# A batched matrix product with x loaded one group ahead, wide stores, and a group's two halves multiplied in two phases

## The chip, the cores and the metric

One core of a Trainium2 chip. The metric is the device time of one execution in microseconds. Kernels are compared with the kernel before on the same chip in the same rounds.

## The reference

```python
batch, dim_i, dim_j, dim_k = 32, 256, 512, 384
x = randn(batch, dim_i, dim_j)      # float32
y = randn(batch, dim_j, dim_k)      # float32
out = np.einsum('bij,bjk->bik', x, y)
```

41.9 MB are read and 12.6 MB written.

## The kernel before

The batch is cut into N = 8 groups of Q = 4 matrices (numbered 0 to 7). Each matrix occupies 32 partitions, so that each partition's data are one long run in HBM: 16 KB of x, 24 KB of y, and for the result 6 KB. Per group:

- VectorE casts x to fp16 and transposes it in 32x32 blocks (pairs of fp16 as one 32-bit word); it casts y in four pieces.
- TensorE multiplies on four row tiles of 32 partitions, one per matrix g. The 256 rows of each result are two halves e (even and odd rows). A group thus has 2 x 4 results of 128x384 fp32, each in one bank of PSUM, the memory that the matmuls write: eight banks, all there are.
- ScalarE copies the banks to SBUF, the memory that the stores read, where the rows get their place for the store. For the last group, VectorE takes half of the copies.

```python
x_pool, y_pool, xt_pool, yr_pool: bufs=2;  xr_pool: bufs=1;  o_pool: bufs=5
psum_pool = tile_pool(name="psum", bufs=2 * Q, space=PSUM)          # 8 banks

def multiply(n):                                                    # ... cut
    for a in range(0, T, 4):                      # four pieces of y, T = 16
        nc.vector.tensor_copy(y_r[:, a:a+4], y_sb[:, a:a+4])
        for e in range(NE):                       # both halves, piece by piece
            for t in range(a, a + 4):
                for g in range(Q):
                    matmul(ps_of[n][e][g], xt[s, e, t // 2, :, t % 2], y_r[s, t],
                           start=(t == 0), stop=(t == T - 1))

def collect(n):                                   # w = 64: 16 copies of 64x384
    for u in range(2):
        for e in range(NE):
            for v in range(2):
                for h in range(2):
                    copy(o[v*w:(v+1)*w, u, h*NE + e], ps_of[n][e][2*u + v][h*w:(h+1)*w])

for n in range(2): load(n)                        # x_n, then y_n
for n in range(N):
    transpose_x(n); multiply(n); collect(n)
    if n + 2 < N: load(n + 2)
    if 0 <= n - 1 and n + 2 < N: store(n - 1)     # two stores of 768 KB
for n in range(N - 3, N): store(n)
```

Every engine runs its instructions in the order of the program, and all transfers go through one queue in that order.

## Time and profile before

| kernel before | |
|---|---|
| time, median of 6 runs | 137.06 us (136.16 to 138.03) |
| profiled span | 135.5 us |
| DMA, VectorE, TensorE, ScalarE busy | 96%, 62%, 47%, 43% |
| data moved | 54.7 MB at 404 GB/s, 54.5 of them through the one queue |

(The prediction had the first three of these runs, median 136.62.) Two of the page's groups; the columns are busy time and the mean of one in ns, then the engine's idle time before it and what ended most of that.

```profile
L113 PE MATMUL o_ps<-y_r,xt_sb 32*128 32x384 f16 x1024 | 64.2, 415 | 62.9 <-DVE y_r L107 61.0
L139 ACT COPY o_sb<-o_ps 64x384 f32<-64x384 f32 x120 | 56.7, 473 | 71.6 <-PE o_ps L113 45.5
```

ScalarE spends 0.47 us on a copy and is idle for more than half of the span. TensorE waits for casts, and for ScalarE hardly at all: 1.8 us in the list of waits.

### The profile page before, as it was taken

How to read it: one execution, taken by the hardware profiler on the slowest of the kernel's cores; microseconds unless marked ns; L12 is line 12 of the kernel's file. 1: busy time of each engine (PE TensorE's matmuls, PEld its weight loads, DVE VectorE, ACT ScalarE, POOL GpSimd, SP SyncE). 2: the span in 40 equal slices, each digit the busy share in tenths (PEclk: the TensorE clock that was granted, in tenths of full speed). 3: DMA queues.
4: the chain of work that ended last, by engine and by line, in shares of the span. 5: the costliest groups of instructions: out<-in, count | busy, mean ns of one | idle time of the engine just before them, and what ended most of it. 6: DMA issues, size and time to landing. Idle time of an engine off the chain costs nothing.

```text
span 135.5 us, 2381 instructions
## 1 busy us (share of the span) xinstructions
PE 64.2 (47%) x1024; PEld 33.7 (25%) x1024; DVE 83.6 (62%) x80; ACT 58.0 (43%) x121; POOL 0.2 (0%) x4
## 2 busy tenths in 40 slices
PE   0000099309934793579408940099302970089500
PEld 0000056104612361136104520045101540045200
DVE  0049777947897596822979059670796509990660
ACT  3000000894089408940794079500795039800640
POOL 0000000000000000000000000000000000000000
PEclk9999999975797579757975698556985698556985
DMA  4999999999999998999999999999999999999765
GB/s 111 426 431 457 414 445 450 389 428 474 392 435 421 435 399 339 442 441 450 398 399 453 423 457 385 415 431 457 418 385 417 441 409 419 415 421 426 302 279 210
DMA packets 5050, 54.68 MB, mean 404 GB/s; under 512 B 560, under 2 KB 560, under 8 KB 3120
## 3 DMA queue, kind: packets, MB, share of 16 engines
q1 hardware_dynamic: 5040, 54.53, 96.2%
q8 instruction: 8, 0.13, 0.4%
q14 instruction: 2, 0.02, 0.0%
HBM read 41.94 MB, written 12.58 MB: 402 GB/s over the span
## 4 chain that ended last, share of the span: by engine, by line
DMA 76%; DVE 13%; PE 5%; SPq 1%; issue 1%; DVEq 1%
DMA x_sb<-in_x_dram 76%; DVE x_r L83 7%; PE o_ps L113 5%; DVE xt_sb L96 3%; DVE o_sb L137 3%; DVE y_r L107 1%; DVEq L192 0%; SPq L77 0%; SPq L67 0%; DVEq L83 0%; DVEq L137 0%; DVEq L96 0%
## 5 line engine op out<-in xcount | busy, mean ns | idle before, releaser
L113 PE MATMUL o_ps<-y_r,xt_sb 32*128 32x384 f16 x1024 | 64.2, 415 | 62.9 <-DVE y_r L107 61.0
L139 ACT COPY o_sb<-o_ps 64x384 f32<-64x384 f32 x120 | 56.7, 473 | 71.6 <-PE o_ps L113 45.5
L113 PEld LDWEIGHTS <-xt_sb 32*128 32x128 f16 x1024 | 33.7, 116 | 93.0 <-DVE y_r L107 46.6
L83 DVE CAST x_r<-x_sb 128x4096 f16<-128x4096 f32 x8 | 18.4, 2294 | 33.3 <-DMA x_sb<-in_x_dram 33.3
L107 DVE CAST y_r<-y_sb 128x1536 f16<-128x1536 f32 x32 | 28.5, 953 | 8.6 <-DMA y_sb<-in_y_dram 8.6
L96 DVE STREAM_TRANSPOSE xt_sb<-x_r 128x512 f32<-128x512 f32 x32 | 32.4, 1072 | 0.7
L137 DVE COPY o_sb<-o_ps 64x384 f32<-64x384 f32 x8 | 4.4, 556 | 5.0 <-PE o_ps L113 4.8
L139 ACT ACT_TABLE_LOAD x1 | 1.3, 1283 | 0.7 <-PEq L181 0.7
L181 POOL MEMSET const-bfloat16-1.0<- 128x1 bf16 x1 | 0.1, 101 | 0.0
L181 POOL MEMSET const-uint8-127<- 128x1 uint8 x1 | 0.1, 101 | 0.0
L181 POOL MEMSET const-float32-0.0<- 128x1 f32 x1 | 0.1, 99 | 0.2 <-issue 0.2
L181 POOL MEMSET const-float32-1.0<- 128x1 f32 x1 | 0.1, 98 | 0.0
## 6 DMA issues: line engine op xcount, KB each, us to landing
y_sb<-in_y_dram SPq DMA_DIRECT2D x7, 3072.0 KB, 25.5
x_sb<-in_x_dram SPq DMA_DIRECT2D x8, 2048.0 KB, 24.9
out_dram<-o_sb SPq DMA_DIRECT2D x16, 768.0 KB, 20.6
y_sb<-in_y_dram SPq DMA_DIRECT2D x4, 768.0 KB, 24.1
```

What stands on the lines that cost most here:

```text
L83: keep(nc.vector.tensor_copy(x_r, x_of.pop(n)))
L96: keep(nc.vector.transpose(dst[:, b, e], src[:, b, e]))
L107: keep(nc.vector.tensor_copy(y_r[:, a : a + step], y_sb[:, a : a + step]))
L113: nc.tensor.matmul(ps_of[n][e][g], xt[s, e, t // 2, :, t % 2], y_r[s, t], start=(t == 0), stop=(t == T - 1),)
L137: keep(nc.vector.tensor_copy(dst, src))
L139: keep(nc.scalar.copy(dst, src))
L181: nc = _bacc.Bacc("TRN2", target_bir_lowering=False, num_devices=1)
```

## The change

Its intent: get the transposes of x off the end of the kernel, and halve the number of packets of the stores. Three things change.

1. *x one group ahead.* The queue gets x of group n+3 before y of group n+2, and VectorE transposes group n+1 before it casts y of group n.
2. *12 KB stores for groups 0 to 5 ("wide").* All eight rows of a partition lie together; for that the copies are 32x384, 32 of them per group: 28 on ScalarE, the 4 of the last bank on VectorE.
3. *Two phases for the wide groups.* Half e=0 is multiplied over the whole of y, then e=1, and each half's four banks are copied when it is done. Groups 6 and 7 stay narrow and mixed, as before.

```diff
     def width(n):
-        return NARROW
+        return WIDE if n < N - 2 else NARROW
@@ the main loop (cut: load, multiply and collect are only split into parts)
-    for n in range(2):
-        load(n)
+    load_x(0); load_x(1); load_y(0); transpose_x(0); load_x(2); load_y(1)
     for n in range(N):
-        transpose_x(n)
-        multiply(n)
-        collect(n)
-        if n + 2 < N:
-            load(n + 2)
+        if n + 1 < N:
+            transpose_x(n + 1)
+        if n > 0 and width(n - 1) == WIDE:
+            collect(nc.vector.tensor_copy, n - 1, NE - 1, Q - 1)
+        round_y(n)
+        if width(n) == WIDE:
+            for e in range(NE):
+                multiply(n, e, 0, T)
+                for g in range(Q):
+                    if (e, g) != (NE - 1, Q - 1):
+                        collect(nc.scalar.copy, n, e, g)
+        else:
+            for a in range(0, T, STEP):
+                for e in range(NE):
+                    multiply(n, e, a, a + STEP)
+            ... # the copies of before, on VectorE for v == 1 of the last group
+        if n + 3 < N:
+            load_x(n + 3)
+        if n + 2 < N:
+            load_y(n + 2)
             ... # store(n - 1) as before
```

More of the change, by code (lines that the diff above doesn't have):

```diff
@@ L5 @@
 from concourse import bass_utils, mybir
-from concourse.masks import make_identity
 from concourse._compat import with_exitstack
@@ L19 @@
 DEFER = 3
+STEP = 4
 @with_exitstack
@@ L58, in width, with load_x @@
     def width(n):
-        return NARROW
-    def pieces(n):
-        return 4
-    def load(n):
+        return WIDE if n < N - 2 else NARROW
+    def load_x(n):
         x_of[n] = x_pool.tile([P, R, J], F32, name="x_sb")
@@ L71, in load, with load_y @@
         )
+    def load_y(n):
         y_of[n] = y_pool.tile([P, T, K], F32, name="y_sb")
@@ L96, in transpose_x, with round_y @@
                     keep(nc.vector.transpose(dst[:, b, e], src[:, b, e]))
-    def multiply(n):
-        xt = xt_of.pop(n).bitcast(MM_DT).rearrange("p e t (m c) -> p e t m c", c=2)
+    def round_y(n):
         y_sb = y_of.pop(n)
-        y_r = yr_pool.tile([P, T, K], MM_DT, name="y_r")
-        ps_of[n] = [
-            [psum_pool.tile([P, K], F32, name="o_ps") for _ in range(Q)] for _ in range(NE)
-        ]
-        step = T // pieces(n)
-        for a in range(0, T, step):
-            keep(nc.vector.tensor_copy(y_r[:, a : a + step], y_sb[:, a : a + step]))
-            for e in range(NE):
-                for t in range(a, a + step):
-                    for g in range(Q):
-                        s = slice(g * PQ, (g + 1) * PQ)
-                        keep(
-                            nc.tensor.matmul(
-                                ps_of[n][e][g],
-                                xt[s, e, t // 2, :, t % 2],
-                                y_r[s, t],
-                                start=(t == 0),
-                                stop=(t == T - 1),
-                            )
-                        )
@@ L122, in collect, with multiply @@
-    def collect(n):
+        yr_of[n] = yr_pool.tile([P, T, K], MM_DT, name="y_r")
+        for a in range(0, T, STEP):
+            keep(nc.vector.tensor_copy(yr_of[n][:, a : a + STEP], y_sb[:, a : a + STEP]))
+    def multiply(n, e, first, last):
+        xt = xt_of[n].bitcast(MM_DT).rearrange("p e t (m c) -> p e t m c", c=2)
+        if first == 0:
+            for g in range(Q):
+                ps_of[n, e, g] = psum_pool.tile([P, K], F32, name="o_ps")
+        for t in range(first, last):
+            for g in range(Q):
+                s = slice(g * PQ, (g + 1) * PQ)
+                keep(
+                    nc.tensor.matmul(
+                        ps_of[n, e, g],
+                        xt[s, e, t // 2, :, t % 2],
+                        yr_of[n][s, t],
+                        start=(t == 0),
+                        stop=(t == T - 1),
+                    )
+                )
@@ L123, in collect @@
+    def collect(copy, n, e, g):
         w = width(n)
         per = P // w
-        o_of[n] = o_pool.tile([P, R, K], F32, name="o_sb")
+        ps = ps_of.pop((n, e, g))
         o = o_of[n].rearrange("p (u f) k -> p u f k", u=Q // per)
-        for u in range(Q // per):
-            for e in range(NE):
-                for v in range(per):
-                    g = u * per + v
-                    ps = ps_of[n][e][g]
-                    on_vector = n == N - 1 and g % 2 == 1
-                    for h in range(per):
-                        src = ps[h * w : (h + 1) * w]
-                        dst = o[v * w : (v + 1) * w, u, h * NE + e]
-                        if on_vector:
-                            keep(nc.vector.tensor_copy(dst, src))
-                        else:
-                            keep(nc.scalar.copy(dst, src))
@@ L140, in collect @@
-        del ps_of[n]
+        for h in range(per):
+            keep(copy(o[g % per * w : (g % per + 1) * w, g // per, h * NE + e], ps[h * w : (h + 1) * w]))
     def store(n):
@@ L153, in store @@
             )
-    for n in range(2):
-        load(n)
-    for n in range(N):
-        transpose_x(n)
-        multiply(n)
-        collect(n)
+    load_x(0)
+    load_x(1)
+    load_y(0)
+    transpose_x(0)
+    load_x(2)
+    load_y(1)
+    for n in range(N):
+        if n + 1 < N:
+            transpose_x(n + 1)
+        if n > 0 and width(n - 1) == WIDE:
+            collect(nc.vector.tensor_copy, n - 1, NE - 1, Q - 1)
+        o_of[n] = o_pool.tile([P, R, K], F32, name="o_sb")
+        round_y(n)
+        if width(n) == WIDE:
+            for e in range(NE):
+                multiply(n, e, 0, T)
+                for g in range(Q):
+                    if (e, g) != (NE - 1, Q - 1):
+                        collect(nc.scalar.copy, n, e, g)
+        else:
+            for a in range(0, T, STEP):
+                for e in range(NE):
+                    multiply(n, e, a, a + STEP)
+            for u in range(2):
+                for e in range(NE):
+                    for v in range(2):
+                        on_vector = n == N - 1 and v == 1
+                        collect(nc.vector.tensor_copy if on_vector else nc.scalar.copy, n, e, 2 * u + v)
+        if n + 3 < N:
+            load_x(n + 3)
         if n + 2 < N:
-            load(n + 2)
-        if n + 2 - DEFER >= 0 and n + 2 < N:
-            store(n + 2 - DEFER)
+            load_y(n + 2)
+            if n + 2 - DEFER >= 0:
+                store(n + 2 - DEFER)
     for n in range(N - DEFER, N):
```

## The prediction

> **What bounds the kernel now.** I read the page first: the slices (part 2), the queues (part 3) and the chain of waits (part 4); then the timeline of the last 35 us.
>
> ```profile
> DMA  4999999999999998999999999999999999999765
> q1 hardware_dynamic: 5040, 54.53, 96.2%
> DMA 76%; DVE 13%; PE 5%; SPq 1%; issue 1%; DVEq 1%
> ```
>
> The reader is to see that the 16 DMA engines are busy from the second slice to the 37th, that the one queue fills 96.2% of their span, and that the chain is three quarters transfers. Only the head (2 us) and the last three slices (3.4 us each; 0.3 + 0.4 + 0.5 of one missing, some 4 us) hold idle DMA. So what can be won is small: the tail, and cheaper packets. What can be lost is larger: anything that makes compute follow the last loads later.
>
> ```profile
> 102.90 0.47 ACT L139 COPY o_sb<-o_ps 64x384 f32<-64x384 f32 x1
> 103.17 3.57 DVE L107 CAST y_r<-y_sb 128x1536 f16<-128x1536 f32 x4 [1.10 <-DMA y_sb<-in_y_dram]
> ...
> 104.19 6.87 PE L113 MATMUL o_ps<-y_r,xt_sb 32*128 32x384 f16 x128 [8.06 <-DVE y_r L107]
> 110.48 7.83 ACT L139 COPY o_sb<-o_ps 64x384 f32<-64x384 f32 x16 [7.11 <-issue]
> 111.82 2.29 DVE L83 CAST x_r<-x_sb 128x4096 f16<-128x4096 f32 x1 [5.09 <-DMA x_sb<-in_x_dram]
> 114.22 4.03 DVE L96 STREAM_TRANSPOSE xt_sb<-x_r 128x512 f32<-128x512 f32 x4
> 118.18 3.52 DVE L107 CAST y_r<-y_sb 128x1536 f16<-128x1536 f32 x4
> 119.15 7.91 PE L113 MATMUL o_ps<-y_r,xt_sb 32*128 32x384 f16 x128 [8.09 <-DVE y_r L107]
> 126.48 3.88 ACT L139 COPY o_sb<-o_ps 64x384 f32<-64x384 f32 x8 [8.18 <-issue]
> 126.54 4.56 DVE L137 COPY o_sb<-o_ps 64x384 f32<-64x384 f32 x8 [4.84 <-PE o_ps L113]
> ```
>
> This is the tail: groups 6 and 7 (counted from 0). ScalarE empties group 6 from 110.48 to 118.31; group 7's matmuls start at 119.15, held by VectorE (cast x, transpose, cast y), and only 0.8 us after the banks are free. From ScalarE's first copy of group 7 (126.48) to the end of the span (135.5) it is 9.0 us: copies to 131.1, the last store issued at 131.16, landed at 134.42, 1.06 us to finish.
>
> ```profile
> 44.64 0.47 PE L113 MATMUL o_ps<-y_r,xt_sb 32*128 32x384 f16 x1 [0.33 <-ACT o_sb L139]
> ...
> 45.62 6.48 PE L113 MATMUL o_ps<-y_r,xt_sb 32*128 32x384 f16 x109 [0.51 <-ACT o_sb L139]
> ...
> 51.33 7.83 ACT L139 COPY o_sb<-o_ps 64x384 f32<-64x384 f32 x16 [5.76 <-PE o_ps L113]
> ```
>
> Here, in an early group, the other regime shows itself: TensorE waits bank by bank for ScalarE, the last 109 matmuls start when the last of eight banks is copied (45.57), and ScalarE's next group begins 5.76 us after that. I use this number below.
>
> **What the Trainium skill says.** "DMA: Bandwidth & Descriptors", section "Why small descriptors are slow (HBM only)": each packet carries a fixed overhead. The trace's packet records agree: medians of 234 ns at 6,144 B, 611 at 16,384 and 912 at 24,576 fit 0.0368 ns per byte plus 8 ns. "PSUM — Partial Sum Buffer", section "Terms": one matmul output fits at most one of eight banks. Here each of a group's eight outputs takes one, so a group that mixes its halves fills all of PSUM; the waits at 44.64 and 45.62 agree. "ScalarE: Activation LUTs", section "What ACT_TABLE_LOAD costs": 186 ns + 0.833 N for an instruction with immediates, back-to-back ones overlapping by some 93 ns, with no term for partitions. For N = 384 that is 506, or 413 apart; the trace has 473, and 7.83/16 = 489 apart, which I use. So a 32-partition copy should cost what a 64-partition one does. "TensorE: Matmul & The Clock Gate", Part 1: an idle window brings the clock to half. The windows of the trace agree: 16 to 20 matmuls per us at granted clock 0.50, 32 at 1.00.
>
> **The change part by part.**
>
> 12 KB stores, groups 0 to 5. Removed: 6 x 256 = 1,536 packets of 6 KB; added: 768 of 12 KB. Saved: 768 x 8 ns / 16 engines = 0.4 us of DMA time, 0.06 per group. In a full queue this counts, but little.
>
> Copies. A wide group needs 8 outputs x 4 blocks = 32 copies of 32x384 where it had 16 of 64x384. VectorE takes 4 (2.25 us at 556 ns and a gap), ScalarE 28: 28 x 0.489 = 13.7 us, up from 7.83. VectorE per group: 2.3 cast + 4.05 transposes (two of twice the length, taken as the same) + 2.25 + 3.57 = 12.2 us, up from 9.9. DMA per group with stores is 7.5 (y) + 4.9 (x) + 3.7 (store) = 16.1 us, so both fit. The serial chain per group, first y cast 0.97 + matmuls 7.2 + transposes into the xt buffer just freed 4.05 + VectorE's copies 2.25 = 14.5, also fits. About 15 us of transfers remain queued in the worst early group (3), so the DMA stays full. Middle: nothing on the path.
>
> Two phases. They let the 28 copies run under the second half's matmuls, but group 6 is narrow: it mixes halves and uses all eight banks at once.
>
> x one group ahead. It moves x7's cast and transposes (6.3 us) out of the end. But x7 now passes the queue before y6: the transfers from x7 on are x7, y6, store 3, y7, store 4. Working back from y7, which landed at 119.26 (119.0 with the saving): minus 7.5 and 3.7, y6 lands at 107.8 (it was 103.14); minus 7.5, x7 at 100.3.
>
> The tail then goes: VectorE 100.3 + 2.3 + 4.05 + 2.25 (group 5's copies) = 108.9, later than y6's landing. First y6 cast 0.97: group 6's matmuls start at 109.9, against 104.19. ScalarE's copies of it begin some 7.2 later (6.3 to 7.5 in the profile), at 117.1. Group 5's 28 copies may hold them further: y5 cast from about 93 to 94, first half done 4.4 later, 13.7 of copies, done at 111 to 112; plus 5.76 gives 116.9 to 117.9. So 117.1 to 117.9. Group 7 needs all eight banks, and the last is free 7.83 later, at 124.9 to 125.7; +5.76 for matmuls to ScalarE's first copy, 130.7 to 131.5; +9.0 as before: span 139.7 to 140.5. The y7 casts, done by 120, no longer matter. The unprofiled median lies 1.1 above the profiled span (136.62 against 135.5); so 140.8 to 141.6. I predict 141.1 us, 3.3% more.
>
> In one sum: group 6's start +5.7, ScalarE's start on it +6.6 to +7.4, the gap from its last copy to group 7's first (8.17 before: 118.31 to 126.48) -2.4, hence +4.2 to +5.0 us.
>
> **The rivals.**
> A. The DMA stays the bound to the end. Stores 4, 5, 6, 7 would follow y7 without a hole: the slowest engine had landed group 6's at 130.37; plus 2 x 1.85 minus 0.4 gives 133.7, plus 1.06: span 134.7, time 135.8, 0.6% faster. For it: the x chain does leave the end. Against it: it needs group 7's copies by about 128.6, while the banks come free only near 125. This is also about the best that the change can reach, because the slowest engine has hardly a hole before 130.
> B. ScalarE becomes the bound everywhere. If a 32-partition copy cost more (say 0.6 us), a group took 16.8 us, over the 16.1 of DMA; the queue would still be covered for several groups, but group 5's copies would end some 3 us later: 144. Against it: the cost shows no partition term.
> C. Serial waits between VectorE and TensorE (transposes wait for the xt buffer) drain the queue in the middle: 14.5 against 16.1 leaves a margin, but early groups, without stores in the queue, come every 12.4 us of DMA, so VectorE falls some 5 us behind there. With 15 us queued this costs nothing; a miss by more would give 142 to 144.
> D. Warm clock: if TensorE is still at full clock when group 7's main burst starts, its 109 matmuls take about 4 us instead of 6.48: 138.8.
>
> **Range and chances.** A spread of 1 us from y6's landing, 1 from the clock in two bursts, B and C above and D below: 139.0 to 142.8. Over 2% faster would be under 133.9, below even A: 0.03. Within 2% (to 139.35) needs A, or D with an early y6: 0.11. Slower by over 2%: 0.86.
>
> **What would show it.** In the changed profile: group 6's first matmul near 110; ScalarE's copies of it from about 117 to 125; TensorE's wait before group 7's main burst put to ScalarE's copies; a hole in the DMA between some 130 and 135; slices before the 36th as full as now; ScalarE's copies of 32x384 near 473 ns. I am wrong if group 7's matmuls start with their y casts (then A), if y6 lands well before 107, or if DMA idles in the middle (C).

## The result, and the profile after

The changed kernel takes 146.06 us (median of 6 runs, 145.45 to 146.78). The ratio to the kernel before is 1.066 (95% interval 1.060 to 1.072). A ratio here is the mean time of one kernel's runs over that of the other's of the same rounds, so it isn't quite the ratio of the medians. Executions over 1.5% slower than the fastest of the same kernel are left out of the means. Predicted were 141.1 us, 3.3% more; it is twice that.

First, from the page of the changed kernel, the slices, the queue and the chain, to be held against those of before in the prediction, and its copies on ScalarE:

```profile
DMA  5999999999999999999999999999999999155055
...
q1 hardware_dynamic: 4176, 54.53, 89.7%
...
PE 4%; DVE 3%; ACT 1%; DVEq 0%; issue 0%
...
L128 ACT COPY o_sb<-o_ps 32x384 f32<-32x384 f32 (+1 forms) x192 | 90.2, 470 | 46.9 <-PE o_ps L113 30.2
```

The DMA is as full as before up to the 34th of 40 slices (3.6 us each). What is new lies in the last six: a store now and then, and nothing between; the queue's share falls from 96.2% to 89.7%. So nothing was lost in the middle as far as transfers go; the end came late. The chain of waits, three quarters transfers before, now names TensorE, VectorE and ScalarE alone; it was followed back only to 127.8 us, which is why its shares add up to 8%. ScalarE's copies did not get dearer (470 ns against 473), but it now makes 192 of them.

The timeline of the end, in the columns start, duration, engine, line, operation, with the idle time before it and its releaser in brackets:

```profile
95.40 3.56 DVE L102 CAST y_r<-y_sb 128x1536 f16<-128x1536 f32 x4
...
96.51 8.30 PE L113 MATMUL o_ps<-y_r,xt_sb 32*128 32x384 f16 x128 [7.59 <-DVE y_r L102]
...
101.86 13.53 ACT L128 COPY o_sb<-o_ps 32x384 f32<-32x384 f32 x28 [1.98 <-issue]
...
111.28 6.17 DVE L102 CAST y_r<-y_sb 128x1536 f16<-128x1536 f32 x7
...
112.39 1.78 PE L113 MATMUL o_ps<-y_r,xt_sb 32*128 32x384 f16 x18 [7.58 <-DVE y_r L102]
115.45 6.73 PE L113 MATMUL o_ps<-y_r,xt_sb 32*128 32x384 f16 x110 [1.28 <-ACT o_sb L128]
...
121.45 7.82 ACT L128 COPY o_sb<-o_ps 64x384 f32<-64x384 f32 x16 [6.06 <-issue]
...
129.33 6.60 PE L113 MATMUL o_ps<-y_r,xt_sb 32*128 32x384 f16 x109 [0.51 <-ACT o_sb L128]
...
135.22 3.88 ACT L128 COPY o_sb<-o_ps 64x384 f32<-64x384 f32 x8 [5.94 <-issue]
```

Read it backwards. ScalarE's first copy of group 7 is at 135.22; then it is 9.0 us to the end, as before. It waited for the burst of 109 matmuls that began at 129.33, when ScalarE had emptied the eighth bank of group 6 (121.45 + 7.82). y7 had been cast long before: the casts at 111.28 are four of y6 and three of y7. Group 6's own burst of 110 matmuls began at 115.45, when ScalarE had made the last of its 28 copies of group 5 (101.86 + 13.53). Those 28 began 6.5 us after the first cast of y5 at 95.40. From 115.45 on ScalarE and TensorE take turns; all that overlaps is the last 0.7 us of each burst and some 20 matmuls of group 7, which run as single banks come free.

Why 6.5 us? The windows of 1 us over group 5's burst show it; the columns are the stretch and its length, busy us of PE, PEld, DVE, ACT and POOL with the number of instructions that ran in brackets (those begun before the stretch are counted too), then PEclk (the granted clock: the share of full speed at which TensorE was let run), the DMA's busy share and GB/s:

```profile
97.00:98.00 1.00, 1.00 (x19) 0.53 (x12) 1.00 (x2) 0.96 (x3) 0.00 (x0) 0.50 1.03 442
98.00:99.00 1.00, 1.00 (x16) 0.53 (x12) 0.97 (x2) 0.98 (x3) 0.00 (x0) 0.50 1.05 451
...
101.00:102.00 1.00, 1.00 (x20) 0.57 (x16) 0.74 (x1) 0.14 (x1) 0.00 (x0) 0.50 1.08 467
...
103.00:104.00 1.00, 1.00 (x33) 0.67 (x25) 0.00 (x0) 0.96 (x3) 0.00 (x0) 1.00 0.89 381
```

For the first 6 us of the burst the granted clock is 0.50, with 16 to 20 matmuls running in each us; only then comes 1.00 with 33. Four at a time run side by side, so fewer start than the brackets say: by their starts in the trace, 12 to 15 per us at 0.50, and 25 at 1.00. So the whole first phase, 64 matmuls in 5.3 us, runs at half clock.

### The profile page after: what moved, and what is told of

Its sections match the earlier page's. It is cut to its first block, busy times and chain, and to the rows that moved or that the text cites. A ratio compares the mean times of both kernels' runs of the same rounds, so it can differ in the third digit from the quotient of the medians.

```text
span 144.2 us, 2454 instructions
## 1 busy us (share of the span) xinstructions
PE 63.7 (44%) x1024; PEld 35.7 (25%) x1024; DVE 95.7 (66%) x92; ACT 91.5 (63%) x193; POOL 0.2 (0%) x4
## 3 DMA queue, kind: packets, MB, share of 16 engines
q1 hardware_dynamic: 4176, 54.53, 89.7%
## 5 line engine op out<-in xcount | busy, mean ns | idle before, releaser
L128 ACT COPY o_sb<-o_ps 32x384 f32<-32x384 f32 (+1 forms) x192 | 90.2, 470 | 46.9 <-PE o_ps L113 30.2
L113 PEld LDWEIGHTS <-xt_sb 32*128 32x128 f16 x1024 | 35.7, 116 | 99.8 <-issue 63.7
L90 DVE STREAM_TRANSPOSE xt_sb<-x_r 128x1024 f32<-128x1024 f32 x12 | 23.4, 1990 | 10.5 <-PE o_ps L113 10.4
L128 DVE COPY o_sb<-o_ps 32x384 f32<-32x384 f32 (+1 forms) x32 | 17.8, 556 | 17.0 <-PE o_ps L113 16.5
L96 DVE STREAM_TRANSPOSE xt_sb<-x_r 128x512 f32<-128x512 f32 x8 | 8.1, 1070 | 5.8 <-PE o_ps L113 5.8
## 6 DMA issues: line engine op xcount, KB each, us to landing
out_dram<-o_sb SPq DMA_DIRECT2D x6, 1536.0 KB, 22.6
```

Of the source, the lines that this page charges most:

```text
L90: keep(nc.vector.transpose(dst[:, e], src[:, e]))
L96: keep(nc.vector.transpose(dst[:, b, e], src[:, b, e]))
L113: nc.tensor.matmul(ps_of[n, e, g], xt[s, e, t // 2, :, t % 2], yr_of[n][s, t], start=(t == 0), stop=(t == T - 1),)
L128: keep(copy(o[g % per * w : (g % per + 1) * w, g // per, h * NE + e], ps[h * w : (h + 1) * w]))
```

## The experiments

**Theory T**: the banks of PSUM are handed on too late at the end. Group 5's 28 copies hold group 6's matmuls; group 6, mixed, fills all eight banks at once, so its 16 copies hold group 7's matmuls entirely. **Rival R1**: the wide copies and the pace they set in the middle are the loss. **Rival R2**: the order of transfers is, since y6 now comes behind x7.

One table for all runs but the last three: where the trace has ScalarE's first copies of groups 6 and 7 and the main burst of group 7's matmuls, and the time. The main burst is the longest unbroken row of a group's matmuls, mostly 109 of its 128.

| run | ScalarE begins 6 | 7's main burst begins | ScalarE begins 7 | median us | ratio to before (95%) |
|---|---|---|---|---|---|
| before | 110.48 | 119.15 | 126.48 | 137.06 | 1 |
| the change | 121.45 | 129.33 | 135.22 | 146.06 | 1.066 (1.060 to 1.072) |
| a1 x ahead alone | 116.63 | 124.50 | 130.38 | 139.82 | 1.022 (1.014 to 1.030) |
| a2 wide alone | 111.99 | 119.87 | 125.38 | 137.16 | 1.001 (0.994 to 1.007) |
| a3 group 6 shared | 120.11 | 124.81 | 130.46 | 141.10 | 1.033 (1.025 to 1.041) |
| a4 tail in phases | 117.38 | (phases) | (phases) | 135.95 | 0.995 (0.988 to 1.001) |
| b1 TensorE warm | 115.76 | 123.64 | 127.63 | 138.63 (three runs) | 1.015 (1.009 to 1.021) |
| b2 three xt buffers | 117.22 | 125.10 | 130.68 | 141.09 | 1.031 (1.027 to 1.035) |
| b4 group 5 narrow | 119.32 | 127.21 | 132.98 | 143.76 | 1.051 (1.048 to 1.054) |
| c1 warm, 1 to 5 only | 116.17 | 124.04 | 129.47 | 140.26 | 1.027 (1.021 to 1.033) |

All gave correct results, including those with dummy matmuls, whose products are overwritten.

### a1 and a2: each part of the change alone

a1 is the changed kernel with all groups narrow and mixed:

```diff
-        return WIDE if n < N - 2 else NARROW
+        return NARROW
```

> x one group ahead, but all eight groups narrow and mixed as before (16 copies of 64x384). Theory T (the banks are handed on too late at the end: group 5's 28 copies hold group 6, group 6's 16 copies on ScalarE hold all eight banks from group 7): y6 still lands near 107, group 6's matmuls start near 108, ScalarE begins it near 115, last bank free near 123, ScalarE's first copy of group 7 near 129, span near 138, time near 139.5 (about 1.8% over before). Rival R1 (the wide copies and the pace they set in the middle are the whole loss): 137 or less, no slower than before. Rival R2 (the order of transfers, y6 behind x7, is the loss): 144 to 146.

Measured: 139.82 us. T's number was 139.5, R1's 137 or less, R2's 144 to 146. (Its profiled run was the slowest of its four, at 141.14; of the trace, the steps count, not the sum.) In its timeline:

```profile
116.63 7.83 ACT L128 COPY o_sb<-o_ps 64x384 f32<-64x384 f32 x16 [8.98 <-issue]
...
124.50 6.59 PE L113 MATMUL o_ps<-y_r,xt_sb 32*128 32x384 f16 x109 [0.51 <-ACT o_sb L128]
```

Group 7 waits for the eighth bank (116.63 + 7.83) here too, though each copy is a narrow one.

a2 has the wide stores and the two phases, but the order of loads and transposes of before:

```diff
@@ the loads before the loop as in the kernel before (cut)
-        if n + 1 < N:
-            transpose_x(n + 1)
+        transpose_x(n)
@@
-        if n + 3 < N:
-            load_x(n + 3)
         if n + 2 < N:
+            load_x(n + 2)
             load_y(n + 2)
```

> Wide stores, 32 copies and two phases for groups 0 to 5, with the order of loads and transposes of the kernel before. T: y6 lands near 103 again, group 5's ScalarE copies end near 107.6 and hold group 6's matmuls a little, ScalarE begins group 6 near 113.6, ends it near 121.5, begins group 7 near 127.4; span near 136.4, time near 138.1 (0.8% over before). R1 (wide copies are the whole loss): 144 to 146. R2: about 137, as before.

Measured: 137.16 us, no slower than before, 0.9 us less than T had. R1 falls as the whole loss: the wide copies alone cost nothing. R2's number for this run was right, but R2 fails a1. The two parts alone cost 2.2% and 0.1%, together 6.6%: x ahead delays the start of groups 5 and 6, and the wide copies lengthen what group 6 then waits for. With the old order there is slack for it: group 5's copies end at 106.7 there (115.4 in the changed kernel) and hold group 6's matmuls too, but its banks are free at about the time at which VectorE has group 7 ready (main burst at 119.87, against 119.15 before).

### a3 and a4: the banks of the last two groups

a3 gives VectorE half of group 6's copies, behind the casts of y7, which come first:

```diff
-                        on_vector = n == N - 1 and v == 1
+                        on_vector = v == 1
@@ for n == N - 2, between the matmuls and the copies
+                round_y(N - 1)      # and not again in group 7's turn (cut)
```

> The changed kernel with half of group 6's 16 copies on VectorE (y7 is cast ahead of them). T: the last bank of group 6 is free 4.6 us after the first copy starts instead of 7.8, so group 7's main burst starts near 126 instead of 129.3, and the time falls by 3.2 us to about 142.8. R1 and R2 (group 7 is late for another reason than the banks): unchanged, 146.

Measured: 141.10 us, 5 less than the change. The step that the edit touches, from ScalarE's first copy of group 6 to group 7's burst, went from 7.88 to 4.70 us, 3.2 less as expected; the rest came from group 6, which was 1.3 us earlier in this trace without a cause in the edit.

a4 multiplies groups 6 and 7 half by half too, and copies each half's four banks when it is done:

```diff
-            for a in range(0, T, STEP):
-                for e in range(NE):
-                    multiply(n, e, a, a + STEP)
-            for u in range(2):
-                ... # copies in the order of u, e, v
+            for e in range(NE):
+                multiply(n, e, 0, T)
+                for g in range(Q):
+                    on_vector = n == N - 1 and g % 2 == 1
+                    collect(nc.vector.tensor_copy if on_vector else nc.scalar.copy, n, e, g)
```

> The changed kernel with groups 6 and 7 also multiplied half by half, each half's four banks copied as soon as it is done; copies and stores still narrow. T: ScalarE begins group 6 near 117 instead of 121.5, group 7's second half starts when the last bank is free, near 125, with 64 matmuls left instead of 109 and half of the copies done; last store near 131.3; span 135 to 136.5, time near 137.5, 8 us under the changed kernel. R1 and R2 (pace of the middle or order of transfers sets the end): at most 2 us less, 144 to 146.

Measured: 135.95 us, ten less than the change; R1 and R2 allowed two.

```profile
117.38 9.79 ACT L128 COPY o_sb<-o_ps 64x384 f32<-64x384 f32 x20 [1.67 <-issue]
...
121.34 2.78 PE L113 MATMUL o_ps<-y_r,xt_sb 32*128 32x384 f16 x63 [0.66 <-ACT o_sb L128]
...
125.26 2.76 PE L113 MATMUL o_ps<-y_r,xt_sb 32*128 32x384 f16 x61 [0.66 <-ACT o_sb L128]
...
127.92 1.94 ACT L128 COPY o_sb<-o_ps 64x384 f32<-64x384 f32 x4 [0.75 <-PE o_ps L113]
```

Group 7's first half is multiplied while ScalarE still empties group 6's second half, and when the last bank is free at 125.26, 61 matmuls are left, not 109. They take 2.76 us; the granted clock stayed at 1.00 from 116.5 on. The traced execution, the slowest of the four, took 137.17 us, about as expected (137.5). The other three took 135.6 to 136.1; why these were faster no trace shows. The x order and the wide stores are all still in this kernel; so the nine microseconds come from how the last groups use the banks, given that order. T stands.

### b4: the other hold

The changed kernel with group 5 narrow and mixed: `n < N - 3` in `width`.

> The changed kernel with group 5 narrow and mixed too (five wide groups instead of six): 16 copies of 64x384 in place of 28 + 4 of 32x384. T (group 5's 28 copies hold group 6's matmuls until 115.4): its copies run from about 104.2 to 112.0, group 6's burst starts near 112, ScalarE begins group 6 near 118 instead of 121.5; time near 142.6. Rival (group 6's own start, not group 5's copies, matters): 145 to 146.

Measured: 143.76 us, 2.3 less than the change where 3.5 were expected. The hold moved one group up: mixed group 5 now waited for group 4's 28 copies (its main burst starts at 99.87), so its own copies ended at 113.5, not at 112.0. A miss in size that again shows the mixed group, not the number of copies by itself, as what waits.

### b1, b2, c1: why the prediction was too low

Two terms of its sum came out larger: group 5 started at 95.4 instead of 93 to 94, and ScalarE followed 6.5 us after that instead of 4.4. b2 tests the first: with three buffers for the transposed x, VectorE need not wait for the matmuls of two groups before. In the changed kernel's list of waits (us in total, times, longest) these are 16.2 us:

```profile
DVE xt_sb L90 <- PE o_ps L113: 10.4, 4, 3.6
...
DVE xt_sb L96 <- PE o_ps L113: 5.8, 2, 3.2
```

```diff
-    xt_pool = ctx.enter_context(tc.tile_pool(name="xt_pool", bufs=2))
+    xt_pool = ctx.enter_context(tc.tile_pool(name="xt_pool", bufs=3))
```

> The changed kernel with three xt buffers instead of two, so that the transposes of group n+1 don't wait for the matmuls of group n-1 (16 us of VectorE idle in all in the changed kernel). Theory S (this serial chain set the pace of the middle, 14.9 us a group, so VectorE began group 5's y cast at 95.4 though y5 had landed at 90.8): group 5's first y cast near 92.2, ScalarE's first copy of group 6 near 117.7 instead of 121.5, time near 142.2, 3.8 us less. Rival (ScalarE's copies, 13.5 us a group, set the pace and take the gain up): 145 to 146.

Measured: 141.09 us, 1.1 less than expected. In its timeline:

```profile
92.18 3.56 DVE L102 CAST y_r<-y_sb 128x1536 f16<-128x1536 f32 x4
...
98.25 13.54 ACT L128 COPY o_sb<-o_ps 32x384 f32<-32x384 f32 x28 [3.02 <-issue]
...
117.22 7.82 ACT L128 COPY o_sb<-o_ps 64x384 f32<-64x384 f32 x16 [5.44 <-issue]
```

Group 5's first cast of y and ScalarE's first copy of group 6 are both within half a microsecond of what was expected. So the serial wait between VectorE and TensorE cost the changed kernel 5 us, without ever emptying the DMA queue. This wait is part of the pace of the middle, so R1 comes back in part: with x ahead that pace does cost time. The gains of a4, b2 and b1 overlap and can't be added up.

b1 tests the second: 28 dummy matmuls ahead of each group but the first keep TensorE busy, in the bank that the group overwrites anyway.

```diff
+        if n > 0 and e == 0 and first == 0:
+            for i in range(28):
+                matmul(ps_of[n, 0, 0], xt[:, 0, i % TW, :, 0], warm_sb, start=True, stop=True)
         for t in range(first, last):
```

> The changed kernel with 28 dummy matmuls (128x128 by 128x384, of a constant tile) ahead of each group but the first, in the bank that the group overwrites, so that TensorE doesn't idle before a group. Theory W (the missing 2 us from group 5's first y cast to ScalarE's first copy, and much of the 6 us per burst in the tail, are TensorE starting each burst at half clock): granted clock near 1.0 in the bursts, ScalarE starts 4.4 to 4.9 us after the first y cast of a wide group instead of 5.2 to 6.5, a group's matmuls take about 5.6 us instead of 7 to 8, the last 109 matmuls about 3.5 instead of 6.6; in all 7 to 10 us less, time 136 to 139. Rival (the bursts are held by casts or by bank waits, not by the clock): 145 to 147, same durations.

Measured: 138.63 us, the median of three runs (the fourth, 141.18, was slow); 7.4 less, within the expected 136 to 139. For group 5 of this run, the timeline and one of its windows:

```profile
92.56 3.56 DVE L105 CAST y_r<-y_sb 128x1536 f16<-128x1536 f32 x4
...
97.07 13.54 ACT L138 COPY o_sb<-o_ps 32x384 f32<-32x384 f32 x28 [0.17 <-ACT o_sb L138]
```

```profile
94.00:95.00 1.00, 0.96 (x28) 0.53 (x20) 1.00 (x2) 0.96 (x3) 0.00 (x0) 1.00 1.03 442
```

At granted clock 1.00, 28 matmuls run and 20 start in this microsecond, and ScalarE starts 4.5 us after the first cast. Same kernel, same data, only a TensorE that had not idled. The cast itself came 2.8 us earlier too (92.56, against 95.40), so the gain is not that of the second term alone. It is near the lower end of the expected 7 to 10: the last 109 matmuls took 4.71 us where 3.5 were expected, and group 6 still found the clock at 0.50 for 3.4 us. ScalarE, with 13.5 us of copies per group, ran without a pause from 65.85 to 96.9, so it may have become the pace itself; that was not tested.

c1 has the dummies ahead of groups 1 to 5 only (`0 < n < N - 2`), so that the bursts at the end are as cold as in the changed kernel.

> The changed kernel with the dummy matmuls ahead of groups 1 to 5 alone, so that the bursts of groups 6 and 7 start as cold as in the changed kernel. If the prediction missed by the slow first half of the wide groups (through group 5's copies and through the pace of the middle) and by little else, this run does what was predicted of the changed kernel: ScalarE's first copy of group 6 near 116.7 to 117.5, span near 139.5 to 140.3, time near 141.2. Rival (the miss sits in the bursts of the tail): 144 to 146.

Measured: 140.26 us, the prediction's figure less 0.8. ScalarE's first copy of group 6 came at 116.17. Not all of group 5 was warm: the clock fell to 0.50 from 92.9 to 96.3, late in a pause of 5.2 us between the dummies and the first matmul, and ScalarE started 5.4 us after the first cast. So group 5's copies began at 97.48, as the prediction had it (97.4 to 98.4), but with the cast 1 to 2 us earlier and the first half 1.0 longer: that these two cancel is luck. The rival, a miss in the bursts of the tail, falls: with the middle sped up, the tail ran as the prediction had it.

### b3, c2, c3: a version that beats both

b3 is a4, with half of the copies of group 6's second half on VectorE and y7 cast ahead of them (the move of the cast is cut here):

```diff
-                    on_vector = n == N - 1 and g % 2 == 1
+                    on_vector = (n == N - 1 or e == NE - 1) and g % 2 == 1
```

> The run with the last two groups in two phases, and in it half of the copies of group 6's second half on VectorE (y7 cast ahead). The banks come free about 1.9 us earlier, but the stores of the slowest DMA engine are nearly the bound by then: 0.5 to 1 us under that run, time near 135.2. Rival (the end is already set by transfers alone): the same as it, 136.

Measured: 135.46 us, ratio 0.991 (0.987 to 0.995), where about 135.2 was expected. It is 0.5 less than a4; the two intervals overlap, so this step is not shown. It was run again, beside a variant with 6 KB stores throughout, and with them 16 copies per group, none on VectorE in groups 0 to 5:

> The kernel with the last two groups in two phases and half of group 6's second half copied on VectorE, again, unchanged: 135.5, 0.9% under the kernel before, for the comparison with the next.

> The same, with 6 KB stores and 16 copies of 64x384 in all groups, still in two phases. The 12 KB runs are worth 768 x 8 ns / 16 = 0.4 us of DMA time in a kernel whose end is set by transfers: 0.3 to 0.5 us over that run, about 135.9. Rival (the wide stores do something else for it, or cost it something): under 135.3, or over 136.5.

Measured: 135.51 us, ratio 0.990 (0.987 to 0.993); and for 6 KB stores 136.74 us, ratio 0.999 (0.995 to 1.003). The page's slices of the run with 12 KB stores:

```profile
DMA  5999999989999999999999999999999999999992
```

The DMA is full to the 39th slice; there is little left to win in this way. The 1.2 us between the two are more than the expected 0.3 to 0.5, and 136.74 lies where the rival had it (over 136.5): the variants differ by more than the packets, and the runs explain only a part. In the traces, a packet of 12 KB takes 460 ns and two of 6 KB 468, and the last store of group 5 lands on the ninth of the 16 DMA engines at 124.18 against 124.59: 0.4 us, the amount worked out. But in the variant with 6 KB stores VectorE also came later to group 6's copies (119.88, behind the last cast of y7; 119.14 in the other), and the slowest DMA engine lay 3.4 us behind the first one instead of 2.8. How much each of these costs was not separated.

## Why the prediction was wrong

Right, by its own steps:

- The DMA stays full in the middle; y6 lands at 106.6 (107.8 predicted) because x7 is ahead of it; the 32-partition copy costs the same as the 64-partition one; VectorE's work per group is 12.0 us (12.2 predicted).
- The tail: group 6 waits for group 5's copies, group 7 for the eighth bank of group 6, and the DMA has a hole there. From ScalarE's first copy of group 6 to the end the sum had 22.6 us (7.83 + 5.76 + 9.0); measured were 22.75. a3 and a4 show by intervention that this handing-on holds the tail.
- Rivals A (transfers to the end), B (dearer copies) and D (a warm last burst: it took 6.60 us) did not occur. C did, in a form that the prediction took for harmless: VectorE fell behind in the early groups. It named an empty queue as the harm; the queue never emptied, the harm came through the late start of group 5.

The step that failed is the one before: "y5 cast from about 93 to 94, first half done 4.4 later, 13.7 of copies, done at 111 to 112". Two of its terms were mis-sized. One is the first half, 4.4 us. Measured: 6.5 us from the first cast to ScalarE's first copy (101.86 - 95.40), 5.3 of them for 64 matmuls, because the burst begins at granted clock 0.50, where four matmuls start every 0.32 us. The prediction doesn't say where its 4.4 comes from. The 3.57 us of casts and 16 more matmuls at 20 per us would give it; that this was the working is a guess. But its rates, "16 to 20 matmuls per us" at 0.50 and 32 at 1.00, are misread: they are the bracketed counts of windows, which take in matmuls begun before. At 16 to 20 per us, 64 matmuls would take 3.2 to 4.0 us, and the casts would about cover them, as they do in b1 at granted clock 1.00 (3.4 us). At the true 12 they outlast the casts.

The other is the start of the cast. From the first group's cast at 20.96, five steps of the predicted 14.5 us give 93.5; the steps measured 14.9 on average, and the cast came at 95.40. "Middle: nothing on the path" was wrong with it: VectorE's transposes waited 16.2 us in all for TensorE. Their last wait (3.2 us, x7's) also made group 6's first matmul 2.5 us late (112.39, where 109.9 was predicted), but its main burst waited for banks until 115.45 anyway.

The sum, put right: the cast of y5 at 95.4 is 1.4 to 2.4 us later than predicted, the first half 2.1 us longer, the 28 copies 0.2 shorter (13.53), the next burst 0.3 longer (6.06 against 5.76): 3.6 to 4.6 us, and ScalarE began group 6 at 121.45, 3.6 to 4.4 us after the predicted 117.1 to 117.9. The prediction also added 1.1 us from the span to the time; the changed kernel's profiled execution took 1.7 more than its span (145.94 against 144.2), which is another 0.6. b1 brings the 6.5 back to 4.5; b2 brings the cast to 92.2; c1, with the sum of both terms as the prediction had it, lands at 140.26, where it had 141.1.

## What to carry to other kernels

When one unit of work fills all accumulation banks, the copies out of them and the next unit's matmuls exclude each other; near the end of a kernel, where no queue hides it, hand banks on in halves. A change that brings one input forward in a queue that is always full pushes another back: look at what the one pushed back starts. And where work comes in bursts with pauses, take the duration of a burst's *first part* from the starts in its timeline: a window's count takes in what began before it.

## What the Trainium skill lacked or had wrong

- "TensorE: Matmul & The Clock Gate", Part 1, puts the ramp penalty under 1% of a typical kernel's span. The figure is for one ramp, and doesn't fit a kernel that goes cold before every group: here, keeping TensorE busy with dummies took 7.4 of 146 us, 5.1%, because short bursts sat on the chain between casts and copies.
- The same part gives a warm-up budget of some 3.4 us. In the trace of the changed kernel group 5's burst ran for 6.0 us (96.51 to 102.50) before the granted clock rose. The free-running window of 3.4 us that the part also gives agrees: the full stretches at one clock lasted 6.83 or 10.24 us there, two or three windows.
- "ScalarE: Activation LUTs", section "What ACT_TABLE_LOAD costs": its formula gives 506 ns for 384 elements, or 413 apart back to back. The copies from PSUM took 470 to 473 ns on average and started 481 to 484 ns apart (medians): no overlap.
- No page that I found says how far the 16 DMA engines drift apart under a full queue. In the trace of before one transfer's parts landed within 1.2 us of each other at the start and within 3.7 us at the end. Eight instruction fetches of 16 KB, each 0.9 to 1.1 us long, ran among the data; the first (at 26.4 us) falls where the spread goes from 1.1 to 2.1. That they cause all of it is not shown.
